# Index scores of a sparse attention block: four of eight weighted heads summed by diagonal fp32 matmuls on TensorE in place of VectorE

## The chip, the cores and the metric

The kernel runs on one core of one Trainium2 chip. The metric is the device time of that core in microseconds (us). A core has five engines that run at the same time, each with its own queue of instructions: TensorE (PE in the rows; its weight loads are PEld), VectorE (DVE), ScalarE (ACT), GpSimd (POOL) and SyncE (SP, which issues DMAs). An engine works through its queue in order, so an instruction that waits holds up all that stands behind it on its engine.

## The reference, cut to what matters

The whole program is two transformer blocks over 1024 tokens; the change lies in the first one, in the indexer that chooses for each query which 256 keys it attends to.

```python
q_idx = (c_q @ w_qi).reshape(B, T, IDX_HEADS, IDX_DIM)         # 8 heads of 64
w_idx = w_idx * (IDX_HEADS ** -0.5 * IDX_DIM ** -0.5)
...
rel = jax.nn.relu(jnp.einsum('bqhd,bsd->bqhs', qb_idx, k_idx))
score = jnp.einsum('bqh,bqhs->bqs', wb, rel).astype(jnp.float32)
score = jnp.where(key_pos[None, None, :] <= q_pos[None, :, None], score, -jnp.inf)
_, sel = lax.top_k(score, n_sel)                                # n_sel = 256
```

For one block of 128 queries the score of a key is the sum over eight heads of a weight (one number for each query and head) times the relu of a dot product. Blocks 0 and 1 have 256 keys at most and need no choice, so scores are computed for blocks 2 to 7.

## The kernel before, in words

The indexer (`indexer`) walks over the blocks in the order 7, 6, 5, 4, 3, 2. Block b has (b+1)*128 keys, and `scores` (L820) takes them in pieces of at most HF = 512 columns: 512+512, 512+384, 512+256, 512+128, 512 and 384 columns, ten pieces and 4224 columns in all. For each piece it goes through four pairs of heads. For one pair:

- PE computes both heads' dot products, two matmuls for each head (the keys are split into a high part `kkh` and a low part `kkl`), into two banks of PSUM. Three such places go round: `pair` 0, `pair` 1 and banks 4 and 5 (`self.nsc`).
- ACT takes the relu into the tile `relu` (L841 for a `pair` in one instruction, L844 for the two banks in two).
- DVE multiplies by the head's weight `widx` and adds to the score `sc`: the first head by a TENSOR_SCALAR (L854), each other by a SCALAR_TENSOR_TENSOR in the helper `stt` (L344). For the last pair of blocks 7 and 6 (`POOL_PAIRS`) ACT multiplies (L857) and POOL adds (L858).

After each pair the loop lets other work of the block into the program by `fill`: products `h` times `wlo`, `whi` into bank 6 that DVE takes off as `z` (L694), norms (`sq`, `rv`, `ry`, `c`), and for block 5 the index queries of the lower blocks (`qs`).

`select_keys` finds the threshold of the 256 best keys, for blocks 7, 6, 5 together (group 0) and for 4, 3, 2 together (group 1). After statistics of the scores (L884, L885) it makes six rounds: from the bracket `tk_lo`, `tk_hi` DVE works out a threshold `tk_tc` (L919 to L923), ACT counts the keys above it for the blocks 7, 6 and 4 by a Sign with an accumulator (L925, output `mark` in group 0), DVE counts for 5, 3 and 2 (L930), and DVE narrows the bracket (L936 to L939). The rounds of group 0 lie among the scores of blocks 4, 3 and 2, those of group 1 behind the last scores. Behind them come the masks (L961 to L964), the bias tiles, and the attention.

PE works in the order in which the program is written. The instructions of DVE, ACT, POOL and the DMA queues are put in order by a scheduler. All PE matmuls of this kind go through the helper `mm` and so have line L209.

Of the kernel before, what the change touches and what calls it, by code (L numbers as in the profile page):

```python
# [13 lines left out]
F32 = mybir.dt.float32  # L14
# [3 lines left out]
AF = mybir.ActivationFunctionType  # L18
ALU = mybir.AluOpType
# [3 lines left out]
P = 128  # L23
# [3 lines left out]
HF = 512  # L27
# [14 lines left out]
NSLOT = 49  # L42
FILLS = {6: 2, 5: 2}
BIAS_AFTER = 4
POOL_PAIRS = {(7, 3): "act", (6, 3): "act"}
ORDER = "w a10 x x a11 x x a12 w x a13 x a14 x x a15 w a16 a17 a00 a01 a02 a03 a04 a05 a06 a07 q w w"
W_ON_DVE = (1, 3)
# [50 lines left out]
def hs(half):  # L98
    return slice(half * HF, half * HF + HF)
# [11 lines left out]
def bs(i, n=P):  # L111
    return slice(i * n, i * n + n)
# [6 lines left out]
class Core:  # L119
# [231 lines left out]
    def setup(self):  # L351
        nc = self.nc
        self.vec = self.const("vec", [P, NVEC])
        nc.sync.dma_start(self.vec, self.I["vec"])
        self.ident = self.const("ident", [P, P])
        make_identity(nc, self.ident)

        self.turned = self.const("turned", [P, P], F32R)
        t = self.scr("turned")[:, :P]
        nc.gpsimd.memset(t, 0.0)  # L360
        nc.gpsimd.affine_select(t, t, pattern=[[1, P]], compare_op=ALU.not_equal, fill=1.0, base=1 - P, channel_multiplier=1)
        nc.vector.tensor_copy(self.turned, t)
        self.ones = self.const("ones", [P, P])
        nc.vector.memset(self.ones, 1.0)

        self.cmask = self.const("cmask", [P, 2 * P], BF16)
        nc.gpsimd.memset(self.cmask, 0.0)
        nc.gpsimd.affine_select(self.cmask[:, :P], self.cmask[:, :P], pattern=[[1, P]], compare_op=ALU.is_gt,
                                fill=BIG, base=0, channel_multiplier=-1)
        nc.gpsimd.affine_select(self.cmask[:, P:], self.cmask[:, P:], pattern=[[-1, P]], compare_op=ALU.is_ge,  # L370
                                fill=BIG, base=0, channel_multiplier=1)
        self.cm01 = self.const("cm01", [P, 2 * P], BF16)
        nc.gpsimd.memset(self.cm01[:, :P], 0.0)
        nc.gpsimd.tensor_copy(self.cm01[:, P:], self.cmask[:, P:])
        self.big = self.const("big", [P, 1])
        nc.vector.memset(self.big, BIG)
        self.iota9 = self.const("iota9", [P, 9])
        nc.gpsimd.iota(self.iota9, pattern=[[1, 9]], base=0, channel_multiplier=0, allow_small_or_imprecise_dtypes=True)
        self.mod = self.const("mod", [P, 48])
        self.sc, self.nsc = {}, 0  # L380


    def mod_step(self, ch, k):
# [436 lines left out]
    def scores(self, b, kkh, kkl):  # L820

        nc = self.nc
        V = nc.vector
        n = (b + 1) * P
        sc = self.slot(f"sc{b}")
        self.sc[b] = sc
        weight = lambda a, m: self.widx[:, b * 8 + a:b * 8 + a + m]
        for c0 in range(0, n, HF):
            c1 = min(n, c0 + HF)
            m = c1 - c0  # L830
            for hp in range(4):
                self.nsc = (self.nsc + 1) % 3
                ps = [self.pairs[self.nsc][:, hs(j)] for j in range(2)] if self.nsc < 2 else self.banks[4:6]
                for j in range(2):
                    q = self.qs[2 * hp + j, b // 4][:, bs(b % 4 if b > 3 else b - 2)]
                    self.mm(ps[j][:, :m], q, kkl[:, c0:c1], True, False)
                    self.mm(ps[j][:, :m], q, kkh[:, c0:c1], False, True)
                r = self.slot("relu")
                if self.nsc < 2:
                    two = lambda a: a.rearrange("p (j c) -> p j c", j=2)[:, :, :m]  # L840
                    nc.scalar.activation(two(r), two(self.pairs[self.nsc]), AF.Relu)  # L841
                else:
                    for j in range(2):
                        nc.scalar.activation(r[:, j * HF:j * HF + m], ps[j][:, :m], AF.Relu)  # L844
                by = POOL_PAIRS.get((b, hp))
                if by == "pool":
                    two = r.rearrange("p (j c) -> p j c", j=2)[:, :, :m]
                    nc.gpsimd.tensor_tensor(two, two, weight(2 * hp, 2).unsqueeze(2).to_broadcast([P, 2, m]), op=ALU.mult)
                for j in range(2):
                    hd = 2 * hp + j  # L850
                    w = weight(hd, 1)
                    a = r[:, j * HF:j * HF + m]
                    if hd == 0:
                        V.tensor_scalar(sc[:, c0:c1], a, w, None, op0=ALU.mult)  # L854
                    elif by:
                        if by == "act":
                            nc.scalar.activation(a, a, AF.Copy, scale=w)  # L857
                        nc.gpsimd.tensor_tensor(sc[:, c0:c1], sc[:, c0:c1], a, op=ALU.add)  # L858
                    else:
                        self.stt(sc[:, c0:c1], a, w, sc[:, c0:c1], op1=ALU.add)  # L860
                self.free(r)
                yield
        nc.gpsimd.affine_select(sc[:, bs(b)], sc[:, bs(b)], pattern=[[-1, P]], compare_op=ALU.is_ge,
                                fill=FILL, base=0, channel_multiplier=1)
        self.dump(f"sc{b}", sc[:, :n])
# [131 lines left out]
    def bias_tables(self):  # L997
# [4 lines left out]
        nc.sync.dma_start(self.onehot[0:32, 0:384], self.I["onehot"])  # L1002
        for _ in range(BIAS_AFTER):
            yield
# [1472 lines left out]
```

## Time and profile before

| | before |
|---|---|
| median of 3 runs | 2304.39 us (2304.09 to 2309.25) |
| the profiled execution | 2305.76 us, its span 2304.0 us |
| mean granted TensorE clock in the span | 0.962 |
| busy in the span: PE, DVE, ACT, POOL | 2147.1, 1386.2, 1030.9, 871.9 us |

The times of the rows are microseconds from the first instruction of the span. The scores run from 88 to 184, and the stage that chooses the keys ends at about 242. The profiled execution is 1.4 us above the median, so a shift worked out in its rows is added to the median.

### The profile page before, as it was taken

The numbers are of one execution on the slowest core, as the hardware profiler recorded it, in microseconds if no ns is written. First come the engines' busy times: TensorE is split into PE (matmuls) and PEld (weight loads), VectorE is DVE, ScalarE is ACT, GpSimd is POOL, SyncE is SP. The second block draws the span as 40 slices with busy tenths as digits, with TensorE's granted clock in tenths as the row PEclk, the third lists the DMA queues.
The fourth block names the chain that finished last, engine by engine and source line by source line (L and its number), as shares of the span: only waits on it lengthen the run. The fifth ranks groups of instructions, "written<-read, shape, count | busy, mean of one in ns | idle before, by whom it ended". The sixth has DMA issues, their size and how long they took to land. (4 is left out here: it accounts for less than half of the span.)

```text
span 2304.0 us, 28392 instructions
## 1 busy us (share of the span) xinstructions
PE 2147.1 (93%) x10073; PEld 1783.5 (77%) x10073; DVE 1386.2 (60%) x2310; ACT 1030.9 (45%) x1623; POOL 871.9 (38%) x553
## 2 busy tenths in 40 slices
PE   5984799998999999999999999999899999999997
PEld 3764778976788888888788777788777888788886
DVE  8899686788621111123577987685874454643475
ACT  4765556643221221122443476675474444544441
POOL 6335231055357756755433521233511443201002
PEclk8987899998999999999999999999999999999999
DMA  7001131165367667776998431125266776865671
GB/s 286 1 26 36 42 101 37 47 241 202 124 208 246 240 214 244 242 274 251 309 330 297 139 100 55 47 66 172 111 213 216 256 253 230 295 205 187 199 249 55
DMA packets 165442, 405.60 MB, mean 176 GB/s; under 512 B 18441, under 2 KB 19761, under 8 KB 165298
## 3 DMA queue, kind: packets, MB, share of 16 engines
q1 hardware_dynamic: 164144, 399.58, 51.1%
q10 hardware_dynamic: 1154, 4.20, 0.5%
q8 instruction: 79, 1.29, 0.2%
q14 instruction: 65, 0.53, 0.1%
HBM read 292.28 MB, written 111.43 MB: 175 GB/s over the span
## 5 line engine op out<-in xcount | busy, mean ns | idle before, releaser
L209 PE MATMUL pair<-h,whi 128*128 128x512 f32 x1408 | 439.3, 394 | 5.3 <-DVE h L344 5.2
L229 POOL TENSOR_TENSOR wlo<-wraw,whi 128x1024 fp32r<-128x1024 f32 x98 | 244.1, 2496 | 377.3 <-ACT whi L226 262.7
L229 DVE TENSOR_TENSOR wl<-st,wh 128x1024 fp32r<-128x1024 f32 x189 | 246.4, 1326 | 203.0 <-ACT wh L226 156.8
L226 ACT ACTIVATE wh<-st 128x1024 fp32r<-128x1024 f32 x189 | 197.3, 1058 | 301.6 <-PE pair L209 92.0
L209 PEld LDWEIGHTS pair<-h,whi 128*128 128x128 f32 x1408 | 267.9, 191 | 63.8 <-DVE h L344 8.0
L209 PE MATMUL pair<-h,wlo 128*128 128x512 f32 x704 | 277.2, 395 | 19.8 <-ACT h L226 19.8
L226 ACT ACTIVATE whi<-wraw 128x1024 fp32r<-128x1024 f32 x121 | 127.5, 1057 | 291.4 <-POOL wlo L229 127.2
L344 DVE SCALAR_TENSOR_TENSOR t<-pair,vec,t 128x1023 f32<-128x1023 f32 (+1 forms) x42 | 53.8, 1282 | 226.9 <-ACT t L1364 215.3
L209 PEld LDWEIGHTS pair<-h,wlo 128*128 128x128 f32 x704 | 134.0, 191 | 49.4 <-issue 12.9
L209 PE MATMUL pair<-wh,wl 128*128 128x512 f32 x388 | 153.7, 396 | 6.3 <-DVE acc L2304 2.6
L209 PE MATMUL pair<-wl,wh 128*128 128x512 f32 x388 | 152.7, 394 | 0.0
L209 PE MATMUL pair<-wh 128*128 128x512 f32 x388 | 152.5, 393 | 0.0
L209 PE MATMUL bank<-wh,wl 128*128 128x512 f32 x368 | 145.1, 394 | 4.0 <-DVE wl L229 4.0
L209 PE MATMUL bank<-wh 128*128 128x512 f32 x368 | 144.2, 392 | 0.0
L209 PE MATMUL bank<-wl,wh 128*128 128x512 f32 x368 | 144.0, 391 | 0.0
L209 PE MATMUL bank<-u,whi 128*128 128x512 f32 x448 | 139.7, 393 | 0.0
L209 PE MATMUL bank<-fa,wh 128*128 128x512 f32 x448 | 138.2, 390 | 0.0
L2343 POOL TENSOR_TENSOR acc<-acc,grow 128x512 f32<-128x512 f32 x16 | 23.3, 1468 | 293.7 <-ACT sq L2342 293.7
L209 PE MATMUL pair<-fa,wh 128*128 128x512 f32 x320 | 102.5, 402 | 0.0
L1372 DVE TENSOR_TENSOR t<-t,pair 128x1024 f32<-128x1024 f32 x21 | 25.6, 1221 | 122.3 <-PE pair L209 119.9
L209 PEld LDWEIGHTS bank<-u,whi 128*128 128x128 f32 x448 | 85.3, 190 | 17.4
L209 PEld LDWEIGHTS bank<-fa,wh 128*128 128x128 f32 x448 | 84.3, 188 | 17.5
(508 smaller groups left out, 5028.8 us busy)
## 6 DMA issues: line engine op xcount, KB each, us to landing
st<-hs SPq DMA_DIRECT2D x173, 256.0 KB, 4.4
ada<-in_ada_dram SPq DMA_DIRECT2D x48, 512.0 KB, 5.7
wraw<-in_f_in_dram SPq DMA_DIRECT2D x44, 512.0 KB, 3.8
wraw<-in_w_in_dram SPq DMA_DIRECT2D x33, 512.0 KB, 3.6
ra<-in_ff_dram SPq DMA_DIRECT2D x32, 512.0 KB, 4.1
rb<-in_ff_dram SPq DMA_DIRECT2D x32, 512.0 KB, 5.7
st<-td SPq DMA_DIRECT2D x64, 256.0 KB, 3.4
hs<-s SPq DMA_DIRECT2D x54, 256.0 KB, 3.8
```

What stands on the lines that cost most here:

```text
L209: self.nc.tensor.matmul(out, w, x, start=start, stop=stop, **k)
L226: self.nc.scalar.activation(out, src, AF.Copy, **k)
L229: (eng or self.nc.vector).tensor_tensor(out, src, hi.bitcast(F32), op=ALU.subtract)
L344: (eng or self.nc.vector).scalar_tensor_tensor(out, a, s, b, op0=op0, op1=op1)
L1372: nc.vector.tensor_tensor(t, t, pg, op=ALU.mult)
L2343: self.nc.gpsimd.tensor_tensor(a, a, self.grow[:, hs(i)], op=ALU.mult)
```

## The change

The heads 0 to 3 (`DIAGS` = 4) are no longer weighted and added on DVE. For each block ACT makes four 128x128 diagonal matrices `diag`, the identity times the weight of one head (24 activations in all). For each piece PE adds up heads 0 to 3 in PSUM by four fp32 matmuls, with a diagonal as the weights and the `relu` tile as the moving operand, into bank 4 or 5 in turn (`acc`). `sums` issues the two matmuls of a pair of heads behind the dot products of the next pair. DVE adds heads 4 to 7 as before, the first of them (head 4) onto `acc` in PSUM. Because banks 4 and 5 now hold the sums, the dot products go round two places, `pair` 0 and `pair` 1, where they had three, and all relus are instructions over both heads.

```diff
--- before.py
+++ after.py
@@ -42,6 +42,8 @@
 NSLOT = 49
 FILLS = {6: 2, 5: 2}
 BIAS_AFTER = 4
+
+DIAGS = 4
 POOL_PAIRS = {(7, 3): "act", (6, 3): "act"}
 ORDER = "w a10 x x a11 x x a12 w x a13 x a14 x x a15 w a16 a17 a00 a01 a02 a03 a04 a05 a06 a07 q w w"
 W_ON_DVE = (1, 3)
@@ -377,7 +379,7 @@
         self.iota9 = self.const("iota9", [P, 9])
         nc.gpsimd.iota(self.iota9, pattern=[[1, 9]], base=0, channel_multiplier=0, allow_small_or_imprecise_dtypes=True)
         self.mod = self.const("mod", [P, 48])
-        self.sc, self.nsc = {}, 0
+        self.sc, self.nsc, self.nacc = {}, 0, 4
 
 
     def mod_step(self, ch, k):
@@ -825,41 +827,49 @@
         sc = self.slot(f"sc{b}")
         self.sc[b] = sc
         weight = lambda a, m: self.widx[:, b * 8 + a:b * 8 + a + m]
+        diag = self.slot("diag", F32, (P, DIAGS, P))
+        for hd in range(DIAGS):
+            nc.scalar.activation(diag[:, hd], self.ident, AF.Copy, scale=weight(hd, 1))
         for c0 in range(0, n, HF):
             c1 = min(n, c0 + HF)
             m = c1 - c0
+            self.nacc = 9 - self.nacc
+            acc = self.banks[self.nacc][:, :m]
+            wait = []
+
+            def sums():
+                for hd, r, a in wait:
+                    self.mm(acc, diag[:, hd], a, hd == 0, hd == DIAGS - 1)
+                    if hd % 2:
+                        self.free(r)
+                wait.clear()
+
             for hp in range(4):
-                self.nsc = (self.nsc + 1) % 3
-                ps = [self.pairs[self.nsc][:, hs(j)] for j in range(2)] if self.nsc < 2 else self.banks[4:6]
+                self.nsc = 1 - self.nsc
+                ps = [self.pairs[self.nsc][:, hs(j)] for j in range(2)]
                 for j in range(2):
                     q = self.qs[2 * hp + j, b // 4][:, bs(b % 4 if b > 3 else b - 2)]
                     self.mm(ps[j][:, :m], q, kkl[:, c0:c1], True, False)
                     self.mm(ps[j][:, :m], q, kkh[:, c0:c1], False, True)
+                sums()
                 r = self.slot("relu")
-                if self.nsc < 2:
-                    two = lambda a: a.rearrange("p (j c) -> p j c", j=2)[:, :, :m]
-                    nc.scalar.activation(two(r), two(self.pairs[self.nsc]), AF.Relu)
-                else:
-                    for j in range(2):
-                        nc.scalar.activation(r[:, j * HF:j * HF + m], ps[j][:, :m], AF.Relu)
-                by = POOL_PAIRS.get((b, hp))
-                if by == "pool":
-                    two = r.rearrange("p (j c) -> p j c", j=2)[:, :, :m]
-                    nc.gpsimd.tensor_tensor(two, two, weight(2 * hp, 2).unsqueeze(2).to_broadcast([P, 2, m]), op=ALU.mult)
+                two = lambda a: a.rearrange("p (j c) -> p j c", j=2)[:, :, :m]
+                nc.scalar.activation(two(r), two(self.pairs[self.nsc]), AF.Relu)
                 for j in range(2):
                     hd = 2 * hp + j
                     w = weight(hd, 1)
                     a = r[:, j * HF:j * HF + m]
-                    if hd == 0:
-                        V.tensor_scalar(sc[:, c0:c1], a, w, None, op0=ALU.mult)
-                    elif by:
-                        if by == "act":
-                            nc.scalar.activation(a, a, AF.Copy, scale=w)
+                    if hd < DIAGS:
+                        wait.append((hd, r, a))
+                    elif (b, hp) in POOL_PAIRS:
+                        nc.scalar.activation(a, a, AF.Copy, scale=w)
                         nc.gpsimd.tensor_tensor(sc[:, c0:c1], sc[:, c0:c1], a, op=ALU.add)
                     else:
-                        self.stt(sc[:, c0:c1], a, w, sc[:, c0:c1], op1=ALU.add)
-                self.free(r)
+                        self.stt(sc[:, c0:c1], a, w, acc if hd == DIAGS else sc[:, c0:c1], op1=ALU.add)
+                if 2 * hp >= DIAGS:
+                    self.free(r)
                 yield
+        self.free(diag)
         nc.gpsimd.affine_select(sc[:, bs(b)], sc[:, bs(b)], pattern=[[-1, P]], compare_op=ALU.is_ge,
                                 fill=FILL, base=0, channel_multiplier=1)
         self.dump(f"sc{b}", sc[:, :n])
```

The change also moves instructions. The first place is on ACT, at the relus of block 3. In these rows `mark` is a count of group 0 over the scores of block 7 (1024 columns) or 6 (896), and the relus belong to block 3. Before:

```order
L841 ACTIVATE relu_1206<-pair_70 128x1024
L841 ACTIVATE relu_1224<-pair_71 128x1024
L844 ACTIVATE relu_1241<-bank_72 128x512
L844 ACTIVATE relu_1241<-bank_73 128x512
L925 ACTIVATE mark_1058,tk_tc_137_1036<-sc_87_619,tk_tc_137_1036 128x1024
L925 ACTIVATE mark_1058,tk_tc_137_1036<-sc_97_724,tk_tc_137_1036 128x896
L841 ACTIVATE relu_1260<-pair_70 128x1024
```

The marks in these rows are those of the third round; those of the rounds 4 to 6 stand behind the last relu of block 2. With the change:

```order
L857 ACTIVATE relu_1220<-pair_71 128x1024
L857 ACTIVATE relu_1238<-pair_70 128x1024
L935 ACTIVATE mark_1068,tk_tc_141_1046<-sc_87_619,tk_tc_141_1046 128x1024
L935 ACTIVATE mark_1068,tk_tc_141_1046<-sc_98_726,tk_tc_141_1046 128x896
L857 ACTIVATE relu_1255<-pair_71 128x1024
L935 ACTIVATE mark_1068,tk_tc_141_1046<-sc_87_619,tk_tc_141_1046 128x1024
L935 ACTIVATE mark_1068,tk_tc_141_1046<-sc_98_726,tk_tc_141_1046 128x896
L793 ACTIVATE sq_1483<-z_635,shb 128x512
L857 ACTIVATE relu_1273<-pair_70 128x1024
```

Here the marks are those of the rounds 5 and 6: all six rounds of marks, twelve instructions, now stand ahead of the last relu of block 3, and the last of them between two relus of that block. Before, six of the twelve stood ahead of it and six behind.

The second place is on DVE, at the end of group 0's rounds. `mark` is DVE's count over block 5 (768 columns), `sc_163` (before) and `sc_160` (with the change) are the scores of blocks 2 and 3. Before, around the fourth round's count:

```order
L344 SCALAR_TENSOR_TENSOR sc_163_1270<-relu_1310,widx,sc_163_1270 128x384
L930 TENSOR_SCALAR mark_1059,tk_tc_137_1036<-sc_109_844,tk_tc_137_1036 128x768
L286 SCALAR_TENSOR_TENSOR rs_t_187_1403<-ry_2_186_1401 128x4
L694 TENSOR_TENSOR z_733<-bank_74,R_396 128x512
L344 SCALAR_TENSOR_TENSOR sc_163_1270<-relu_1310,widx,sc_163_1270 128x384
```

With the change, around the sixth round's count:

```order
L933 TENSOR_TENSOR tk_tc_141_1046<-tk_lo_142_1047,tk_u_148_1067 128x3
L940 TENSOR_SCALAR mark_1069,tk_tc_141_1046<-sc_111_849,tk_tc_141_1046 128x768
L960 COPY tk_top_228_1607<-tk_tc_141_1046 128x3
L346 SCALAR_TENSOR_TENSOR sc_160_1210<-relu_1255,widx,bank_73 128x512
L346 SCALAR_TENSOR_TENSOR sc_160_1210<-relu_1255,widx,sc_160_1210 128x512
```

The sixth round's count stands ahead of the first DVE sum of block 3; before, the fourth count stood at the last sums of block 2, and the last two behind them.

The third place is PE at the first piece of block 4. `qs` are the index queries of one head. Before:

```order
L209 MATMUL bank_72<-kkl_599,qs_571 128x512
L209 MATMUL bank_72<-kkh_598,qs_571 128x512
L209 MATMUL bank_73<-kkl_599,qs_571 128x512
L209 MATMUL bank_73<-kkh_598,qs_571 128x512
L209 MATMUL pair_70<-kkl_599,qs_582 128x512
```

With the change:

```order
L211 MATMUL pair_70<-kkh_598,qs_571 128x512
L211 MATMUL pair_70<-kkl_599,qs_571 128x512
L211 MATMUL pair_70<-kkh_598,qs_571 128x512
L211 MATMUL bank_73<-relu_1028,diag_1019 128x512 x2
L211 MATMUL pair_71<-kkl_599,qs_582 128x512
```

Two fp32 matmuls on the relu of the pair before now stand between the dot products of one pair and the next, and the third place for dot products is gone.

## Rows read from the trace of the kernel before

**Rows 1.** Stretches of time: length, busy us (instructions) by engine, PE clock, DMA

```profile
core 0: us, PE busy (x) PEld busy (x) DVE busy (x) ACT busy (x) POOL busy (x), PEclk, DMA share, GB/s
88.00:184.00 96.00, 72.72 (x324) 58.66 (x323) 90.14 (x199) 63.43 (x105) 33.41 (x27) 0.86 0.08 23
184.00:242.00 58.00, 32.93 (x150) 26.67 (x150) 55.70 (x182) 30.09 (x55) 31.70 (x22) 0.74 0.09 28
500.00:1000.00 500.00, 485.33 (x2117) 400.90 (x2116) 171.44 (x189) 117.64 (x126) 303.76 (x191) 0.98 0.64 216
```

**Rows 2.** The same view: scores of blocks 7 to 5, then of 4 to 2

```profile
88.00:137.50 49.50, 42.44 (x205) 34.84 (x205) 45.24 (x88) 32.48 (x52) 15.05 (x14) 0.97 0.00 1
137.50:168.70 31.20, 24.90 (x97) 20.10 (x96) 29.60 (x82) 22.35 (x41) 9.71 (x8) 0.73 0.04 7
```

**Rows 3.** Groups of DVE instructions by shape, 88 to 184: busy, mean ns

```profile
L344 DVE SCALAR_TENSOR_TENSOR sc<-relu,widx,sc 128x512 f32<-128x512 f32 x36 | 30.8, 856 | 2.1 <-ACT relu L841 0.5
L344 DVE SCALAR_TENSOR_TENSOR sc<-relu,widx,sc 128x384 f32<-128x384 f32 x12 | 11.8, 987 | 0.2
L854 DVE TENSOR_SCALAR sc<-relu,widx 128x512 f32<-128x512 f32 x6 | 3.0, 495 | 1.9 <-ACT relu L844 1.9
```

**Rows 4.** PE in order of time: start, us, instruction, [wait before it]

```profile
95.48 0.39 PE L209 MATMUL bank<-kkh,qs 128*128 128x512 f32 x1
95.71 0.39 PE L209 MATMUL bank<-kkl,qs 128*128 128x512 f32 x1
...
143.45 1.05 PE L340 MATMUL bank<-ident,ry 128*128 128x128 f32 x8
144.26 0.31 PE L209 MATMUL bank<-kkl,qs 128*128 128x128 f32 x1
...
171.69 0.81 PE L1007 MATMUL bank<-onehot,relb 32*8 32x384 f32 x2
172.42 0.50 PE L209 MATMUL bank<-h,wlo 128*128 128x512 f32 x1
```

**Rows 5.** The same view: PE's four longest waits in blocks 7 to 5

```profile
103.47 0.50 PE L209 MATMUL bank<-h,wlo 128*128 128x512 f32 x1 [0.80 <-DVE z L694]
...
114.64 0.50 PE L209 MATMUL bank<-h,wlo 128*128 128x512 f32 x1 [2.00 <-DVE z L694]
...
126.92 0.39 PE L209 MATMUL bank<-cz,wql 128*128 128x256 f32 x1 [2.29 <-DVE qs L229]
...
135.08 1.05 PE L330 MATMUL bank<-ones,sq 128*128 128x1 f32 x8 [1.27 <-DVE qs L229]
```

**Rows 6.** Groups of ACT instructions by shape, 88 to 184

```profile
L841 ACT ACTIVATE relu<-pair 128x1024 f32<-128x1024 f32 x16 | 16.3, 1025 | 6.6 <-PE pair L209 6.6
L791 ACT ACTIVATE sq<-z,shb 128x512 f32<-128x512 f32 x8 | 5.6, 720 | 2.3 <-DVE tk_over L936 1.2 <-DVE z L694 0.9 <-POOL sc L858 0.2
L226 ACT ACTIVATE whi<-wraw 128x1024 fp32r<-128x1024 f32 x3 | 3.2, 1058 | 0.8 <-DMA wraw<-in_w_v_dram 0.4 <-DMA wraw<-in_w_qk_dram 0.3
L844 ACT ACTIVATE relu<-bank 128x128 f32<-128x128 f32 x4 | 0.9, 271 | 0.0
```

**Rows 7.** ACT in order of time: the marks of the second round

```profile
155.47 1.15 ACT L925 ACTIVATE mark<-sc,tk_tc 128x1024 bf16<-128x1024 f32 x1 [4.61 <-DVE tk_tc L923]
...
157.64 0.61 ACT L226 ACTIVATE c<-z 128x512 fp32r<-128x512 f32 x1
```

**Rows 8.** DVE in order of time: three sums, group 1's first and sixth count

```profile
143.64 0.75 DVE L344 SCALAR_TENSOR_TENSOR sc<-relu,widx,sc 128x512 f32<-128x512 f32 x1
...
174.89 2.54 DVE L344 SCALAR_TENSOR_TENSOR sc<-relu,widx,sc 128x384 f32<-128x384 f32 x1
...
183.16 0.61 DVE L344 SCALAR_TENSOR_TENSOR sc<-relu,widx,sc 128x384 f32<-128x384 f32 x1
...
190.47 0.76 DVE L930 TENSOR_SCALAR_CACHE_REDUCE pair<-sc,tk_tc 128x512 f32<-128x512 f32 x1
...
217.55 0.75 DVE L930 TENSOR_SCALAR_CACHE_REDUCE pair<-sc,tk_tc 128x512 f32<-128x512 f32 x1
```

**Rows 9.** POOL in order of time

```profile
171.64 7.99 POOL L229 TENSOR_TENSOR wlo<-wraw,whi 128x1024 fp32r<-128x1024 f32 x3
```

## The prediction

> **What bounds the kernel now.** I read the stretches of time first. From 88 to 184, while the scores are computed, DVE is busy 90.1 of 96.0 us, PE 72.7, ACT 63.4 [rows 1]: DVE is the fullest engine, and that invites taking work off it. From 500 on PE is busy 485 of 500, and the order there is the same before and after, so what moves the end of the stage at 242 moves the end of the kernel one to one. Split, the stage shows two kinds of stretch [rows 2]. In the blocks 7 to 5 PE is already busy 42.4 of 49.5 us; it waits 0.80, 2.00, 2.29 and 1.27 us for DVE [rows 5], 6.4 us together, at a mean granted clock of 0.97 of the upper level (2.4 GHz). In the blocks 4 to 2 the clock is 0.73, about half of the time at the lower level (1.2 GHz), ACT has 22.4 us of work in 31.2, with idle time such as the 4.61 us before a mark that waits for a threshold from DVE [rows 7]. The scores end with DVE's last sum at 183.16 + 0.61 = 183.8; group 1's first count is at 190.47 and its sixth at 217.55 [rows 8]. These three points carry the sum.
>
> **What leaves DVE.** 40 instructions over 4224 columns: 6 TENSOR_SCALAR and 18 SCALAR_TENSOR_TENSOR of 512 columns, 8 instructions of 384, 8 of 256 and 128. At 0.495 and 0.856 the first 24 cost 18.4 us; the eight of 384 at most 0.987 each, 7.9; the others some 3 [rows 3]. That is 29 us; with the undisturbed 0.75 [rows 8] and the small ones in proportion 24. The means are high because some sums run beside POOL: one of 384 columns takes 2.54 us [rows 8] while three POOL instructions run from 171.64 to 179.63 [rows 9]; an undisturbed one takes 0.61. I take 24 us.
>
> **What comes to PE.** Forty fp32 matmuls, 4 x 4224 = 16,896 columns, 33 times 512. No fp32 matmul of 512 columns is in the trace. Nearest: four of 128 take 144.26 - 143.45 = 0.81 us, so 0.81 for 512 columns if it goes with the width; one of 384 takes 172.42 - 171.69 = 0.73, so 0.97 at most [rows 4]. I take 0.85, nearer the first, which is at the higher clock and steady: 33 x 0.85 = 28 us (27 to 32). One score matmul of 512 takes 95.71 - 95.48 = 0.23, so a sum costs nearly four of them. The Trainium skill, "FP8 and Floating Point Precision", TensorE Precision Notes, says that true FP32 takes four passes through the array; 4 x 0.23 = 0.92 would make it 30 us. The rows at 0.81 and 0.97 lie around that.
>
> **Blocks 7 to 5.** They have 2688 of the columns, 21 times 512: 21 x 0.85 = 17.9 us for PE. PE's own work was 49.5 less the 6.4 of waits and some 3 of shorter gaps, 40 us. With 58 us of work and waits of 3 us left (DVE loses about 15 of its 45 us, so most waits close) the stretch takes 61 us and ends at 149, where it ended at 137.5: **+11.5**. DVE's relief is worth only the 3 to 7 us of closed waits here; PE pays 18 for it. The 12 diagonals of these blocks and the relus fit beside that: ACT has 32.5 us in 49.5 [rows 2].
>
> **Blocks 4 to 2.** PE needs here about 10 us more than the 24.9 that it was busy (at a clock of 0.73) [rows 2], DVE has 9 us less; neither is the limit. ACT's order is: all twelve marks of group 0 now stand ahead of the last relu of block 3, and ACT takes its queue in turn. Its work from 149 to the last relu of block 2: 8 relus of 1024 at 1.0 = 8.2, 4 of 768 at three quarters = 3.1, 4 of 256 at about 0.4 = 1.5; six pairs of marks at 157.64 - 155.47 = 2.17 [rows 7] = 13.0; 8 diagonals at 0.27, the price of a 128x128 relu [rows 6] = 2.2; 4 `c` at 0.61 [rows 7] = 2.4; 5 `sq` at 0.72 and one `whi` at 1.06 [rows 6] = 4.7. Sum 35 us. Before the first mark the thresholds have to be made from block 5's last sum, a chain that PE can't fill because two places for dot products are soon full; later marks wait less, since relus stand between them. I take 5 us of such waits, about one of 4.61 [rows 7] (bounds: 1 if relus cover all, 12 if three rounds wait so long). The last relu then ends at 149 + 40 = 189, the last sum 1.5 us later (two sums of 384 and the way to them): 190.5, **+6.7** on 183.8. So four of the 11.5 come back, because half of the marks have left the stretch behind.
>
> The 24 diagonals cost ACT 24 x 0.27 = 6.5 us in all; they count only where ACT is the limit, and those are in the 35. If ACT had no slack in blocks 7 to 5 either, 12 x 0.27 = 3.2 us more would show.
>
> **The tail.** Group 1's first count came 6.7 us after the last sum, with the last rounds of group 0 and the last `z` between. The rounds are gone from there (a count at 1.0, its small instructions 1.2: 2.2 us), but the five `h` products that stand behind the last dot products on PE end about 5 us after these, and the `z` that takes the last of them off stands on DVE ahead of the thresholds of group 1. It ends at 195 to 196, and the first count comes at 197: again **+6.5**. From the first to the sixth count 217.55 - 190.47 = 27.1 us passed, with group 0's sixth round in it; without this (2.5 us) it is 24.6, so the sixth count is at 221.6, **+4**. Masks, bias and attention follow in the same order. POOL's 8 us [rows 9] can now fall on other DVE instructions than before; the price was about 2 us for each one hit (2.54 against 0.61), and I leave it even. The Trainium skill, "SBUF — State Buffer", SBUF: two separate sides, says that a DVE instruction with two inputs in SBUF and a GpSimd instruction exclude each other; the sum of head 4, whose second input lies in PSUM, would be exempt by that, and the 2.54 us agrees with the first half.
>
> The profiled execution of before, 2305.8, would become 2309.8; on the median 2304.4 + 4 = **2308.4 us**. What a measurement can tell from no change is 0.3%, 6.9 us, so this is no change that can be told.
>
> **Rivals.**
> 1. DVE was the limit, and its relief arrives. For it: 90.1 of 96 us busy. Then the end comes down by up to 24 us, to 2280, or by half of that, 2292, if PE takes back part, or by less still, as below. Against it: PE can't be done with blocks 7 to 5 before 88 + 58 = 146, 8.5 us later than before, so the gain would have to come from ACT without waits (146 + 36 = 182, sums at 183.5) and from a tail freed of group 0: rounds of group 1 that take 4 us less and start 4 us earlier give 8 to 10 us, 2295. Chance 0.16.
> 2. ACT's queue becomes a shuttle: each mark waits for DVE's threshold, the relus behind it wait, and PE waits with both places full. It decides where three of the six rounds wait as long as 4.61 us: +7 over my 5. With fp32 sums at 0.97 in blocks 7 to 5 (21 x 0.12 = 2.5) the end is at +4 + 7 + 2.5 = +13.5: 2318. For it: before, a relu seldom stood behind a mark that waited; now the last four stand so. Against: DVE has 9 us less to do there and answers sooner. Chance 0.26.
> 3. The two cancel, and nothing of the change is seen at the end because the stage ends where PE's and ACT's losses meet group 0's earlier rounds: 2304. It can't be told from my forecast in the time, but in the trace: the last sum would stand at 184 to 186. Chance 0.14.
>
> **How the numbers follow.** My forecast (2304 to 2314) has 0.44; rival 3 overlaps it. Low end: rival 1's smaller form, 2295; its larger forms, down to 2280, are left out with 0.1. High end: rival 2 with the waits at their bound, +4 + 7 + 4 (all 33 x 0.12) = +15, and 2 for one more DVE instruction under POOL: 2321, with 0.07 left above it. Range 2295 to 2321; the forecast's own is 2304 to 2314. Faster by over 0.3% (under 2297.5): rival 1 and a little, 0.19. Slower (over 2311.3): rival 2 and the upper part of the forecast, 0.37. The rest, 0.44, is no change.
>
> **What would show it.** In the trace after: PE busy over nine tenths of the scores of blocks 7 to 5, at the higher clock, ending near 149 (right) or before 143 (the fp32 sums are cheaper than 0.81); an fp32 sum at 0.81 to 0.97 from start to start; DVE with idle time from 88 to 184; ACT nearly gapless from 149 to 189, with marks that wait for `tk_tc`; DVE's last sum near 190; group 1's counts from 197 to 222. Wrong would be: a last sum before 184, or rounds of group 1 without long instructions, which ends below 2300; or waits of over 3 us before most marks, which ends above 2315.

## The result and the profile after

The changed kernel takes 2320.41 us (median of 7 runs, 2314.17 to 2326.47) against 2304.69 (7 runs, 2299.94 to 2313.89): a ratio of 1.0063 with a 95% interval of 1.0044 to 1.0082, so it is slower by 15.7 us. That is inside the range (2295 to 2321), at its upper end, and outside of the forecast's own (2304 to 2314). The profiled execution has a span of 2317.0 us (before 2304.0).

The same stretches in the trace after: the blocks 7 to 5 from the first dot product to the first one of block 4, then to the end of the dot products, then from the last sum to the end of the masks.

```profile
core 0: us, PE busy (x) PEld busy (x) DVE busy (x) ACT busy (x) POOL busy (x), PEclk, DMA share, GB/s
87.50:151.75 64.25, 61.32 (x251) 44.48 (x251) 28.43 (x73) 36.66 (x60) 13.49 (x14) 0.96 0.00 1
151.75:197.30 45.55, 35.42 (x129) 24.58 (x129) 35.62 (x106) 32.86 (x59) 9.60 (x9) 0.83 0.04 13
201.75:260.80 59.05, 33.50 (x154) 27.15 (x152) 57.59 (x160) 28.24 (x49) 37.15 (x24) 0.77 0.13 36
```

Against [rows 2] DVE has turned from the fullest engine (45.2 of 49.5) to the emptiest but POOL (28.4 of 64.3), and PE is busy 61.3 of 64.3. Both stretches have become longer by 14 to 15 us. The price of a sum, from PE in order of time (an fp32 sum counts as two instructions in these rows, so that x4 is two sums):

```profile
105.18 0.39 PE L211 MATMUL pair<-kkh,qs 128*128 128x512 f32 x1
105.41 1.88 PE L211 MATMUL bank<-relu,diag 128*128 128x512 f32 x4
106.72 0.79 PE L211 MATMUL bank<-h,wlo 128*128 128x512 f32 x1
107.35 0.63 PE L211 MATMUL bank<-h,whi 128*128 128x512 f32 x2
```

Two sums start at 105.41, the next matmul at 106.72, and the one behind that 0.63 us later, where two such matmuls start 0.23 us apart without a sum ahead of them [rows 4]: the two sums take 1.31 + 0.40 = 1.71 us, 0.86 each. In the blocks 4 to 2, on PE and on ACT:

```profile
166.04 1.16 PE L342 MATMUL bank<-ident,ry 128*128 128x128 f32 x8 [3.69 <-ACT sq L806]
...
173.48 0.82 PE L211 MATMUL bank<-relu,diag 128*128 128x128 f32 x4 [2.70 <-ACT relu L857]
...
191.74 0.44 PE L211 MATMUL pair<-kkl,qs 128*128 128x384 f32 x1 [1.52 <-ACT relu L857]
```

```profile
161.16 1.02 ACT L857 ACTIVATE relu<-pair 128x1024 f32<-128x1024 f32 x1 [2.32 <-PE pair L211]
...
168.67 1.15 ACT L935 ACTIVATE mark<-sc,tk_tc 128x1024 bf16<-128x1024 f32 x1 [2.42 <-DVE tk_tc L933]
...
194.75 0.81 ACT L857 ACTIVATE relu<-pair 128x768 f32<-128x768 f32 x1 [1.19 <-PE pair L211]
...
197.18 1.06 ACT L228 ACTIVATE whi<-wraw 128x1024 fp32r<-128x1024 f32 x1 [1.61 <-DMA wraw<-in_w_v_dram]
198.14 0.80 ACT L857 ACTIVATE relu<-pair 128x768 f32<-128x768 f32 x1
```

PE waits for an `sq` and a `relu` that stand on ACT behind marks; ACT waits for a threshold, and at other times for dot products that stand on PE behind fp32 sums. So the waits go both ways. The view of ACT's waits from 151.75 to 198.94, the end of the last relu, has them added up (us in total, times, the longest):

```profile
ACT mark L935 <- DVE tk_tc L933: 5.5, 4, 2.4
ACT relu L857 <- PE pair L211: 5.1, 5, 2.3
```

The tail, on DVE and POOL:

```profile
198.97 2.78 DVE L346 SCALAR_TENSOR_TENSOR sc<-relu,widx,sc 128x384 f32<-128x384 f32 x2 [1.56 <-ACT relu L857]
...
202.67 2.26 DVE L285 TENSOR_SCALAR rs_t<-tk_var 128x3 int32<-128x3 int32 x1
...
204.96 2.26 DVE L286 TENSOR_SCALAR tk_std<-rs_t 128x3 int32<-128x3 int32 x1
...
211.84 0.75 DVE L940 TENSOR_SCALAR_CACHE_REDUCE pair<-sc,tk_tc 128x512 f32<-128x512 f32 x1
...
235.25 0.75 DVE L940 TENSOR_SCALAR_CACHE_REDUCE pair<-sc,tk_tc 128x512 f32<-128x512 f32 x1
```

```profile
202.55 4.65 POOL L231 TENSOR_TENSOR wlo<-wraw,whi 128x1024 fp32r<-128x1024 f32 x2 [0.43 <-ACT whi L228]
```

The last sum ends at 201.75 (before 183.77), group 1's counts run from 211.84 to 235.25 (before 190.47 to 217.55 [rows 8]), and the masks end at 260.8 (242). Two instructions over three columns, which as a rule take 0.16, take 2.26 us each beside POOL's `wlo`; before, the `wlo` of this stretch lay beside the last sums [rows 8, 9].

### The profile page after: what moved, and what is told of

It reads as the page before. It is cut to its first block, busy times and chain, and to the rows that moved or that the text cites. A ratio compares the mean times of both kernels' runs of the same rounds, so it can differ in the third digit from the quotient of the medians.

```text
span 2317.0 us, 28507 instructions
## 1 busy us (share of the span) xinstructions
PE 2172.8 (94%) x10153; PEld 1796.0 (78%) x10153; DVE 1362.6 (59%) x2270; ACT 1038.6 (45%) x1634; POOL 865.8 (37%) x553
## 5 line engine op out<-in xcount | busy, mean ns | idle before, releaser
L211 PE MATMUL pair<-h,wlo 128*128 128x512 f32 x704 | 276.7, 395 | 18.7 <-ACT h L228 18.6
```

Of the source, the lines that this page charges most:

```text
L211: self.nc.tensor.matmul(out, w, x, start=start, stop=stop, **k)
```

## The experiments

All times below stand against runs of the kernel before on the same chip, whose medians were 2302.7 to 2306.6 us. Because the scores begin at 87.4 to 88.1 in some traces and at 91.3 to 91.6 in others, points of the stage are given in us after the first dot product. The table holds, from the rows of DVE and PE in each trace: group 0's first threshold (the start of `tk_tc`), the end of DVE's last sum, the start of group 1's first count, and the stage's end (the start of `tk_bad`).

| kernel | threshold | last sum | first count | end | ratio to before (95%) |
|---|---|---|---|---|---|
| before | 55.4 | 95.7 | 102.4 | 154.2 | |
| changed | 67.5 | 114.3 | 124.3 | 173.4 | 1.0063 (1.0044 to 1.0082) |
| sums left out | 53.4 | 86.6 | 99.9 | 149.0 | not comparable |
| one-pass sums | 54.2 | 90.6 | 100.7 | 150.2 | 0.9973 (0.9951 to 0.9994) |
| before, two places | 62.5 | 95.8 | 102.4 | 153.2 | 0.9984 (0.9971 to 0.9996) |
| late rounds | 66.2 | 106.6 | 119.4 | 170.1 | 1.0048 (1.0027 to 1.0070) |
| sums in 7, 6, 5 | 67.4 | 107.8 | 114.5 | 166.1 | 1.0019 (1.0000 to 1.0038) |
| sums in 4, 3, 2 | 52.9 | 102.8 | 112.7 | 163.7 | 1.0012 (0.9995 to 1.0030) |
| sums in 3, 2 | 57.4 | 98.8 | 109.0 | 157.0 | 0.9993 (0.9974 to 1.0013) |
| one-pass, splits on DVE | 54.8 | 89.3 | 99.1 | 148.3 | 0.9901 (0.9869 to 0.9934) |
| the same, again | 54.9 | 89.0 | 98.6 | 148.0 | 0.9942 (0.9925 to 0.9959) |
| before, splits on DVE | 56.4 | 96.9 | 103.4 | 153.7 | 1.0018 (1.0002 to 1.0034) |
| changed, splits on DVE | 67.7 | 114.0 | 122.7 | 172.5 | 1.0062 (1.0040 to 1.0085) |
| one-pass, six heads | 57.1 | 97.9 | 107.3 | 156.3 | 0.9986 (0.9969 to 1.0002) |

The theory was that PE pays for the fp32 sums where it was near its limit, and that ACT's marks, all ahead of block 3's last relu, hold the rest. The rivals were the lost third place, and steps other than the four passes.

**Sums left out.** Heads 0 to 3 are missing from the scores.

```diff
-                    self.mm(acc, diag[:, hd], a, hd == 0, hd == DIAGS - 1)
...
+                    elif hd == DIAGS:
+                        V.tensor_scalar(sc[:, c0:c1], a, w, None, op0=ALU.mult)
```

> The 40 fp32 sums are left out, so the scores lack heads 0 to 3; DVE starts with head 4. Diagonals, two places and DVE's relief stay. Theory (PE pays for the sums in blocks 7 to 5, and ACT's marks hold the relus in blocks 4 to 2): the first score matmul of block 4 comes at 134 to 138 where it was at 151.8 with the sums, the last DVE sum at 178 to 186, the time at 2295 to 2304. Rival (the fp32 sums cost little, the two places or the diagonals do it): block 4 still starts after 145 and the time stays above 2312.

The dot products of block 4 begin at 137.3, in the range of the theory, and the last sum ends at 174.4, 3.6 us ahead of its range. The time, 2660.23 us, can't be used: with these scores the selection's flag sends the program through an exact search, in which DVE works almost alone from 250 to 620 (busy 357 of 370 us). The stage can. DVE has all of its relief here (its sums fall from 56.7 to 19.3 us) and PE none of the sums, and yet the stage ends only 5.2 us earlier than before, though the last sum ends 9.1 us earlier:

```profile
173.84 0.59 DVE L346 SCALAR_TENSOR_TENSOR sc<-relu,widx,sc 128x384 f32<-128x384 f32 x1
174.35 2.35 DVE L285 TENSOR_SCALAR rs_t<-rv 128x4 int32<-128x4 int32 x1
...
177.02 2.24 DVE L286 TENSOR_SCALAR ry<-rs_t 128x4 int32<-128x4 int32 x1
...
179.34 2.21 DVE L288 SCALAR_TENSOR_TENSOR rs_t<-ry 128x4 f32<-128x4 f32 x1
...
187.71 0.75 DVE L941 TENSOR_SCALAR_CACHE_REDUCE pair<-sc,tk_tc 128x512 f32<-128x512 f32 x1
```

From the last sum to the first count 13.3 us pass, where it was 6.7: the threshold chain now lies beside POOL's `wlo` (174.09 to 181.5 in this trace), and three instructions over four columns take 2.2 to 2.4 us.

**One-pass sums.** The diagonals and the relus of heads 0 to 3 are rounded to the format that a matmul takes in one pass.

```diff
-        diag = self.slot("diag", F32, (P, DIAGS, P))
+        diag = self.slot("diag", F32R, (P, DIAGS, P))
-                r = self.slot("relu")
+                r = self.slot("relu", F32R if 2 * hp < DIAGS else F32)
```

> The sums read diagonals and relus of heads 0 to 3 that are rounded to the one-pass matmul format, so each sum is one pass; the rounding changes the scores a little. Theory: a sum of 512 columns takes about 0.23 us where the fp32 one takes 0.86, which gives 13 us back in blocks 7 to 5; block 4 starts at 138 to 141, the time is 2299 to 2309. Rival (it is the extra steps relu, sum, DVE and not the passes): under 5 us come back, over 2313.

Measured 2300.68 us, in the range of the theory, and 0.3% faster than before, hardly clear of the noise. Two sums of 512 columns and the matmul behind them:

```profile
145.77 0.62 PE L211 MATMUL bank<-relu,diag 128*128 128x512 f32 x2
146.23 0.40 PE L211 MATMUL bank<-h,wlo 128*128 128x512 f32 x1
```

They start 0.46 us apart, 0.23 for each sum, where the fp32 ones took 1.71. The threshold comes 13.3 us earlier than in the changed kernel, as 21 x (0.86 - 0.23) = 13.2 has it, and the blocks 4 to 2 give back another 10.3 or so (from 46.8 to 36.4 between threshold and last sum). The end of the stage moves by 23.2, more than the 19.2 that the change lost: what an fp32 sum takes beyond one pass is shown as the cause in the blocks 7 to 5. In the blocks 4 to 2 the 10.3 holds something else too, since the scheduler let only one relu stand behind the marks of round 5 here, and none behind those of round 6. In the tail, on DVE in order of time, a threshold instruction of four columns again takes 2.26 us:

```profile
186.14 2.26 DVE L290 SCALAR_TENSOR_TENSOR ry<-rs_t,ry 128x4 f32<-128x4 f32 x1
```

**Two places in the kernel before.**

```diff
-                self.nsc = (self.nsc + 1) % 3
+                self.nsc = (self.nsc + 1) % 2
```

> The kernel before with two places for dot products in place of three, all sums on DVE. Theory (places matter little while PE and DVE are the limits): last DVE sum within 4 us of 183.8, time 2302 to 2309. Rival (the lost place is what holds PE and ACT): the last sum comes 8 us later or more, time over 2312.

Measured 2303.79 us; the last sum and the first count are where they were. The threshold comes 7 us later, and PE waits 8.5 us for relus, but DVE, which ran 11 us behind the relus at the end, takes that up. In the kernel before the third place was worth nothing. Whether it would help the changed kernel no run shows; the run without sums has two places as well, and its threshold comes 2 us earlier than before.

**Late rounds.** The rounds 4 to 6 of group 0 need block 2's scores (times zero), so that their marks can't stand among the relus.

```diff
-PICK_EARLY = 11
+PICK_EARLY = 6
...
+            next(pick, None)
             self.fill(ROUND_FILLS[n % 2])
...
+            if r == 3 and not inside:
+                self.stt(t, self.sc[2][:, :nb], 0.0, t, op1=ALU.add)
```

> The changed kernel, but the rounds 4 to 6 of group 0 wait for the last sum of block 2, so that only six marks stand among the relus. Theory (marks that wait for thresholds hold the relus and through them PE): the last sum comes at 188 to 193 where it was at 201.8; the three rounds then lie in the tail, so that the stage gains 0 to 8 us and the time is 2312 to 2320. Rival (PE's fp32 sums alone set the last relu): the last sum stays at 199 or later and the time rises to 2324 or more.

```profile
191.86 2.80 DVE L346 SCALAR_TENSOR_TENSOR sc<-relu,widx,sc 128x384 f32<-128x384 f32 x2 [1.25 <-ACT relu L858]
195.26 0.98 DVE L943 TENSOR_SCALAR_CACHE_REDUCE mark<-sc,tk_tc 128x768 bf16<-128x768 f32 x1
...
206.20 1.01 DVE L943 TENSOR_SCALAR_CACHE_REDUCE mark<-sc,tk_tc 128x768 bf16<-128x768 f32 x1
...
207.41 0.75 DVE L943 TENSOR_SCALAR_CACHE_REDUCE pair<-sc,tk_tc 128x512 f32<-128x512 f32 x1
```

The last sum ends at 194.7 in this trace, 7.1 us earlier (nearly 2 us later than expected), so the marks of the last rounds did hold the relus: between threshold and last sum 40.4 us pass, where it was 46.8 in the changed kernel and 40.3 before. The stage ends only 3.3 us earlier, since the rounds 4 to 6 of group 0 now lie in the tail, the counts of two of them (195.26 and 206.20) ahead of group 1's first. The time is 2317.61 us; its interval overlaps that of the change.

**Sums in some blocks only.** The others are done on DVE with three places, as before.

```diff
-DIAGS = 4
+DIAGS_OF = {7: 4, 6: 4, 5: 4}      # or {4: 4, 3: 4, 2: 4}, or {3: 4, 2: 4}
+PLACES = lambda nd: 2 if nd else 3
```

> The sums on TensorE for the blocks 7, 6 and 5 alone (21 of the 33 times 512 columns); the blocks 4, 3 and 2 are weighted and added on DVE with three places, as before. Theory (PE was near its limit in blocks 7 to 5, so its 21 x 0.86 us show there): group 0's first threshold 66 to 69 us after the first score matmul (before 55.4, changed kernel 67.5), the last DVE sum 8 to 13 us later than before, time 2311 to 2317. Rival (most of the loss arises in blocks 4 to 2): time under 2309.

> The sums on TensorE for the blocks 4, 3 and 2 alone; 7, 6 and 5 on DVE with three places, as before. Theory: group 0's first threshold as before (55 to 57 us after the first score matmul); the last DVE sum 4 us earlier to 6 us later than before, since DVE ran 11 us behind the relus there; time 2301 to 2311. Rival (blocks 4 to 2 lose by themselves, as marks and four-pass sums meet there): last sum 8 us later or more, time over 2312.

> The sums on TensorE for the blocks 3 and 2 alone, 8 fp32 sums, where DVE was 11 us behind the last relu. Theory: the last DVE sum 2 to 8 us earlier than before, of which the tail keeps less than half; time 2299 to 2305. Rival (the sums cost on PE what they give on DVE): 2306 or more.

With the sums in 7, 6 and 5 the threshold comes 12.0 us later than before and all behind it follows: last sum 12.1, end 11.9. With the sums in 4, 3 and 2 the threshold comes 2.5 us early, the last sum 7.1 us late and the end 9.5 late: in the trace the rival was nearer, these blocks lose by themselves, though the time (2309.27 us) stayed in the range of the theory. The stage's losses, 11.9 and 9.5, add up to 21.4, against the 19.2 of the change. With 3 and 2 alone the last sum is 3.1 us late, not early. That fits that rival, but does not show it: all six rounds of group 0 stand ahead of the last sum there, too, and one of the last three sums lies beside a POOL instruction (the three take 3.66 us, undisturbed 1.8). The times, 2311.94, 2309.27 and 2307.73 us, have the same order, but are smaller by some microseconds than the ends of the stage would have it, and the last two can't be told from no change. One of the ten executions with the sums in 7, 6 and 5 took 5494.19 us, for a reason that no trace shows.

**Two weight splits on DVE.** Two of the three `wlo` about the last sums and group 1's first thresholds are made on DVE (1.2 us each, one 2.29) in place of POOL (2.4): with one-pass sums, in the kernel before, in the changed kernel.

```diff
+        self.lo_by = deque([self.nc.vector])
         for b in (7, 6, 5, 4, 3, 2):
```

> The kernel with one-pass sums, and two of the three weight splits wlo that POOL made beside group 1's thresholds are made on DVE (about 1.3 us each). Theory (a DVE instruction caught beside such a POOL instruction takes 2.2 us and more, however small, and so the tail eats what the earlier sums gain): the first count of group 1 comes 2 to 6 us earlier after the first score matmul than with one-pass sums alone (100.7), time 2294 to 2299. Rival (the length of the small instructions has another cause, or DVE pays as much for the splits): first count at 100 or later, time 2300 or more.

> The kernel before with the two weight splits wlo of the stage's end made on DVE in place of POOL. Theory (POOL's long instructions stretch whatever DVE runs beside them, sums before and thresholds after, and that is worth some microseconds in any version): 2296 to 2303, the last DVE sum within 2 us of before. Rival (with DVE as the fullest engine two more instructions of 1.3 us cost what they save): 2304 to 2309.

> The changed kernel with the same two splits on DVE. Theory: the first count of group 1 comes 6 to 7 us after the last DVE sum where it took 10.1; time 2312 to 2318. Rival (the splits have nothing to do with the long way from the last sum to the first count): 9 us or more, time 2319 or more.

> One-pass sums with the two splits on DVE, once more and in more rounds: its stage ended only 2 to 6 us earlier in the trace than that of the one-pass kernel and of the kernel before, but its time was 13 and 19 us less, and the splits alone gave nothing on either kernel. If the stage is all of the gain, the time is 2295 to 2301; if there is a further gain behind the stage, it is again under 2290.

```profile
175.79 0.62 DVE L346 SCALAR_TENSOR_TENSOR sc<-relu,widx,sc 128x384 f32<-128x384 f32 x1
...
186.06 0.75 DVE L942 TENSOR_SCALAR_CACHE_REDUCE pair<-sc,tk_tc 128x512 f32<-128x512 f32 x1
```

In these rows (the second run with one-pass sums) 9.6 us still lie between last sum and first count. The first count comes 1.6 and 2.1 us earlier than with one-pass sums alone, at the lower bound of the theory; in the changed kernel the way from sum to count falls from 10.1 to 8.7 us, not to 6 or 7, and the time (2317.48 us, in the range of the theory) does not change; in the kernel before nothing is gained (2307.16 us), as the rival had it. So small DVE instructions do last longer beside POOL's (see the end), but that moving two splits away pays is shown neither in the kernel before nor in the changed one; that DVE pays nearly as much for the splits as they cost beside it is only argued. The one-pass version with the splits was 2287.70 and then 2294.27 us, so the same kernel differs by 6.6 us between two sets of runs. Its stage ends only 6 us before that of the kernel before; why it gains 11 to 19 is open. It is faster than both kernels, at the price of the rounding.

**Six heads.** One-pass, with the splits on DVE and no pair on POOL.

```diff
-DIAGS = 4
+DIAGS = 6
-POOL_PAIRS = {(7, 3): "act", (6, 3): "act"}
+POOL_PAIRS = {}
```

> Six heads in place of four summed by one-pass sums, the splits on DVE, and no pair of heads on POOL. Theory (with one-pass sums DVE is no longer what the stage waits for, so that more relief is worth little): last DVE sum 0 to 3 us earlier than with four (88.7 us after the first score matmul), time 2283 to 2291. Rival (DVE's work is still worth its time): 6 us or more at the last sum, under 2282.

```profile
184.42 0.34 PE L211 MATMUL pair<-kkh,qs 128*128 128x384 f32 x1
...
188.75 0.62 DVE L346 SCALAR_TENSOR_TENSOR sc<-relu,widx,sc 128x384 f32<-128x384 f32 x1
```

The last dot product with four heads, one-pass sums and the splits on DVE:

```profile
171.59 0.35 PE L211 MATMUL pair<-kkh,qs 128*128 128x384 f32 x1
```

Measured 2302.20 us, and neither had it: the last sum comes nearly 9 us later than with four heads (97.9 against 89.0 to 89.3), because the last dot product does (184.42 less the start at 91.48 is 92.9, with four heads 171.59 less 87.41 is 84.2). Up to there ACT waits 16.9 us for dot products (with four heads 11.6) and PE 9.9 us for relus (6.5). DVE's relief is worth nothing at that point; PE and ACT carry the stage. The run changes two things at once, heads and POOL's pairs, and can't part them.

## Why the prediction was right, and where it was off

The range held by 0.6 us, and the direction of the point was right, but the case that I called likeliest, no change that can be told, did not come. Rival 2's time (2318) came within 2 us, and that is luck: neither of the terms that made it up was measured (waits for thresholds of 12 us in place of 5, and 0.97 for a sum; measured 5.5 and 0.86). Other terms, which the prediction had at nothing, filled the range.

- **A sum's price.** Right: 0.85 taken, 0.86 measured, for 512 columns, 3.7 times the 0.23 of a one-pass sum. The Trainium skill, "FP8 and Floating Point Precision", TensorE Precision Notes, has four passes for true FP32; an estimate by that is 4 x 0.23 = 0.92. The measured price is a little under it.
- **Blocks 7 to 5.** Right in the mechanism, 3 us short in size: block 4's first dot product came at 151.75, where 149 (+11.5) was predicted, 14.3 us later than before. PE is busy 61.3 of 64.3 us and waits some 3, as taken. The short term is PE's other work, taken as 40 us where [rows 2] has it busy 42.4: 42.4 + 18.1 for the sums is 60.5. The threshold comes 12.1 us later after the first dot product. The one-pass run gives 13.3 of it back, so it was the passes.
- **Blocks 4 to 2.** This step failed: +6.7 at the last sum, measured +18.0. ACT's work was right (35 us taken, 34.5 busy from 151.75 to the end of the last relu at 198.94), and so was the size of the waits for thresholds (5 taken; ACT's marks waited 5.5 us for `tk_tc`, four times), though the longest came in the third and fourth round and the first mark waited for nothing. What failed is "neither is the limit", which puts ACT's waits for PE at nothing: ACT waited 5.1 us for dot products that stand on PE behind sums, so that PE's sums and ACT's marks took turns instead of running side by side. The 11.3 us that are missing are these 5.1, the 2.8 from the blocks 7 to 5, 1.6 in which ACT waits for a DMA ahead of a `whi` that stands before the last relu, 1.3 more from the last relu to the last sum, where a sum lies beside POOL, and the 0.5 of `tk_tc`. Between threshold and last sum the change loses 6.5 us (46.8 for 40.3); late marks alone (40.4) or one-pass sums alone (36.4) give all of it back, so their shares can't be added.
- **The tail.** First count 6.5 us behind the last sum predicted, 10.1 measured; the stretched threshold instructions beside `wlo` (2.26 twice), which the prediction left even, are 4 us of it. From first to sixth count 24.6 predicted, 23.4 measured. So +4 became 4 + 11.3 + 3.6 - 1.2 = 17.7 at the sixth count.
- **One to one.** This premise was off as well: the stage ends 18.6 us later, the median rises by 15.7, the span by 13.0. Behind `tk_bad` the profiled execution of before takes 2061.8 us, the changed one 2056.2, and the others, but for the run without sums, between 2050 and 2064. Instructions of ACT that both traces have come 18 us later at 400, 16 to 17 between 600 and 1000, 15.5 to 15.7 between 1200 and 1700, and 12.4 to 13 behind 1800. What sets these microseconds isn't settled.
- **Rival 1**, DVE's relief, fails by the run without sums: with nothing to pay on PE the stage gains 5.2 us, though DVE's sums are 37 us shorter there (the prediction took 24 off DVE; in the changed kernel they fall from 56.7 to 22.8, by 34, what POOL stretches included). The rest goes to waits of DVE, and to the tail, where the earlier thresholds fall beside POOL's splits.

## What to carry to other kernels

The fullest engine of a stretch isn't always what its end waits for: take its work out in a run that leaves it out, and read how far the end moves, before paying for it on another engine. An fp32 matmul of 512 columns cost 3.7 one-pass matmuls here; the sum by diagonals cost time on a TensorE that was already busy 42 of 49 us, and rounded to one pass it paid 0.3% (with two splits on DVE 0.6 to 1%). Where two engines hand tiles to each other with few buffers, ask for the waits of each on the other, and do not put one at nothing because neither engine is full.

## What was not expected of the hardware

DVE instructions over at most four columns, 0.16 us as a rule, took 2.1 to 2.4 us beside a POOL `wlo` of 128x1024 (2.4 us) in eleven of the fourteen traces, that of the kernel before among them, and about 1.2 beside a POOL instruction of 128x512 (1.3). With six heads a 2.35 us one (`tk_std<-rs_t`, at 190.61) ends when the `wlo` does that started 0.05 us ahead of it. Instructions with one input only are among them (`rs_t<-tk_var`, 2.26). The diagonals cost ACT 0.32 us each (24 of them 7.7 us busy), not the 0.27 of a relu of the same size from PSUM. The scores began 3.5 us later in four of the fourteen traces than in the others, with nearly the same instructions ahead of them; in these four PE waits 4.8 us for a `whi` of ACT between 60 and 75, and in none of the others.
